# Keys with high and low part in adjacent DRAM rows, and key and query loads that write 128 partitions at once

## The chip, the core and the metric

The kernel runs on one core of a Trainium2 chip. The metric is the device time of one execution in microseconds (us); the time of a kernel is the median of several executions. The engines named below are TensorE (PE in the profile; its weight loads are PEld), VectorE (DVE), ScalarE (ACT), GpSimd (POOL) and SyncE (SP), which issues all DMA transfers of this kernel. Each engine works through its own list of instructions in order.

## The reference

One step of a one-layer encoder over 2048 prompt tokens and 32 sample tokens, with model width 1024. All of it is in float32. What is computed:

```
z = rmsnorm(x) @ w_in                      # columns: q, k, v of group A, then of group B
group A, 4 heads of 2 maps x 64 dims:      # differential attention, 128-dim values
    s = q.k * 64**-0.5 + t5_bias, chunk-causal mask (chunks of 64)
    w = softmax(s[map 1]) - lam * softmax(s[map 2]);   o = w @ v
group B, 8 heads of 64 dims:               # band attention: own chunk and the 8 before it
    s = q.k * 64**-0.5 + clipped relative bias;        o = softmax(s) @ v
h = x + concat(rmsnorm_per_head(oA) * 0.8, rmsnorm(oB)) @ w_out
h = h + square(relu(rmsnorm(h) @ w_up)) @ w_down
h = h + sigmoid(h @ w_ple_gate) * (p @ w_ple_proj)
y = rmsnorm(h)
```

The sample tokens attend to a cache of 128 keys and values beside their own. Keys and values of both groups are outputs too.

## The kernel before, in words

**Precision.** TensorE multiplies in a float32 format (`float32r`) that keeps fewer bits than float32. Each operand is therefore split in a high part and a low part (`split`, L191 to L202): ScalarE copies the value to the high part, and GpSimd or VectorE subtracts to get the low part. A projection multiplies three times (`mm3`, L235 to L241): high by high, high by low, low by high.

**Attention scores use the split differently.** A key has 64 features, and TensorE contracts over 128 partitions. So one key tile holds the high parts of 64 features in partitions 0 to 63 and the low parts in partitions 64 to 127 (`ka` for group A, `kbt` for group B). The query tile `q` holds the same 64 feature rows twice, once in each half of the partitions, and has the query's high part and its low part side by side in its columns. Two matmuls, one with the high and one with the low columns of the query, then give the score with all four products (L669 for group A, L856 for group B).

**Where keys and queries lie.** The projections (`proj`) write them to DRAM scratch: keys to `kS`, laid out as [head, high or low, 128 feature rows, token], queries to `qS`, as [head, map, 64 feature rows, block of 256 tokens, high or low, token]. `caches` adds the cached keys. Attention loads them back:

- `attn_a` (group A, four heads, called for groups `js` of query blocks) loads per head the keys as tiles of up to 1024 tokens, each by one DMA for the high half and one for the low half, and per query block `q` by two DMAs, one for each half of the partitions (`load_q`).
- `attn_b` (group B, eight heads per group of query blocks) loads per head the keys `kbt` by two DMAs and the queries of two blocks by two DMAs, beside the biases `bb` and the values `vbt`.

Each of these loads writes 64 partitions.

**Order of the work.** The program is written in stages: norm and projections of group A for the first half of the tokens; half of differential attention (`JA0`); projections of group B, with half of band attention (`JB`) within; the rest of the projections and of band attention; the other half of differential attention (`JA1`); output projection (`outproj`, matmuls `ops`), MLP (`ups`, `dps`), gate (`gps`) and final norm, block by block of 512 tokens. A scheduler then orders the instructions of each engine by its own model of their times, with the order of the program as priority: where attention has to wait for VectorE or ScalarE, matmuls of later stages (projections, output projection, MLP) stand in between. The change touches what the scheduler sees of the loads, and so the lists of all engines.

**Around 780 to 975 us** band attention of the last blocks and the output projection of the first 512 tokens run side by side. `outproj` makes 8 output tiles; for each it loads a weight tile (`wr`, split by ScalarE into `wh` and by GpSimd into `wl`), loads the residual (`hd`, from `x_t`), lets TensorE do 24 matmuls into `ops`, lets VectorE add them to `hd` (L992), and stores `hd` to `hS`. `oload` brings in attention's result (`oraw`, from `oT`) for the next block and splits it into `oact` or `ou`.

Of the kernel before, what the change touches and what calls it, by code (L numbers as in the profile page):

```python
# [13 lines left out]
F32 = mybir.dt.float32  # L14
# [6 lines left out]
P = 128  # L21
D = 1024
SP = 2048
SS = 32
T = SP + SS
PAST = 128
KC = SP + PAST + SS
# [130 lines left out]
class Kern:  # L158
# [208 lines left out]
    def scratch(self):  # L367
        self.xT = self.a["x_t"]
        self.pT = self.a["p_t"]
        self.qS = self.dram([8, 2, 64, 9, 2, 256], F32, "qS")  # L370
        self.kS = self.dram([8, 2, P, KC], F32, "kS")
        self.vS = [self.dram([KC, D], F32, "vSa"), self.dram([KC, D], F32, "vSb")]
        self.oT = self.dram([P, 8, T], F32, "oT")
        self.hS = self.dram([P, 8, T], F32, "hS")
        self.rS = self.dram([P, T], F32, "rS")
        self.rB = self.dram([P, T], F32, "rB")
# [112 lines left out]
    def proj(self, half, grp, acts, sg, mm, vs=range(2), gs=range(4)):  # L489
# [8 lines left out]
        for g in gs:  # L498
            gi = 4 * grp + g
            for kind in range(2):  # L500
                wh, wl = self.wunit(a["w_qk"][8 * grp + 4 * kind + g], [8, P])
                for b in half:
# [37 lines left out]
                    for i, t in enumerate((hi, lo)):  # L540
                        for c0, kc, n in self.ktok(b):
                            self.dma(self.kS[gi, i, :, kc : kc + n], t[:, c0 : c0 + n])
                    if grp == 0 or b == 3:
# [6 lines left out]
    def caches(self, sg, tp):  # L550
        nc, a = self.nc, self.a
        for grp in range(2):
# [9 lines left out]
            for i, t in enumerate((hi, lo)):  # L562
                self.dma(
                    self.kS[4 * grp : 4 * grp + 4, i, :, SP : SP + PAST].rearrange("g p c -> p g c"),
                    t.rearrange("p (g c) -> p g c", c=P),
                )
            for c in range(2):
                raw = sg.tile([P, 256], F32, tag="vraw", bufs=2, name="cvr")
                self.dma(raw, cv[:, 256 * c : 256 * c + 256])
                hl = sg.tile([P, nh // 2, 2, dv], F32R, tag="vhl", bufs=2, name="cvhl")  # L570
# [7 lines left out]
    def load_q(self, q, gi, ms, j, n=1):  # L578
        for d in range(2):
            dst = q[64 * d : 64 * d + 64]  # L580
            if j is None:
                for i, m in enumerate(ms):
                    self.dma(dst[:, i, :, :SS], self.qS[gi, m, :, 8, :, :SS])
            elif len(ms) == 2:
                self.dma(
                    dst.rearrange("r m l c -> r m (l c)"), self.qS[gi, :, :, j].rearrange("m r l c -> r m (l c)")
                )
            else:
                self.dma(
                    dst.rearrange("r k l c -> r (k l c)"),  # L590
                    self.qS[gi, ms[0], :, j : j + n].rearrange("r k l c -> r (k l c)"),
                )

    def attn_a(self, js, pool, ps_s, ps_t, ps_o):
        nc = self.nc
        last = 8 in js
        nk = SP if last else 256 * (js[-1] + 1)
        late = []
        for g in range(4):
            q = self.queries(g, js[0], pool)  # L600
            kts = [self.kpool.tile([P, 2, 1024], F32R, tag="ka", bufs=2, name="ka") for _ in range(0, nk, 1024)]
            if last:
                ks = pool.tile([P, 2, PAST + SS], F32R, tag="ks", bufs=1, name="ks")
            for hl in range(2):
                src = self.kS[g, hl].rearrange("(m r) c -> r m c", m=2)
                for i, kt in enumerate(kts):
                    c0, n = 1024 * i, min(1024, nk - 1024 * i)
                    self.dma(kt[64 * hl : 64 * hl + 64, :, :n], src[:, :, c0 : c0 + n])
                if last:
                    self.dma(ks[64 * hl : 64 * hl + 64], src[:, :, SP:KC])  # L610
            ba = self.bias_a(self.qpool, g)
            for j in js:
                self.attn_a_pair(g, j if j < 8 else None, kts if j < 8 else [ks], ba, pool, ps_s, ps_t, ps_o, late, q)
                q = None
# [152 lines left out]
    def attn_b(self, js, pool, ps_s, ps_t, ps_o):  # L767
# [12 lines left out]
        for h in range(8):  # L780
            gi, m = 4 + h // 2, h % 2
            bb = self.bias_b(pool, h)
            kt = pool.tile([P, KBW], F32R, tag="kb", bufs=2, name="kbt")
            for hl in range(2):
                self.dma(kt[64 * hl : 64 * hl + 64, : ke - kb], self.kS[gi, hl, 64 * m : 64 * m + 64, kb:ke])
            q = pool.tile([P, 2, 2, 256], F32R, tag="q", bufs=2, name="q")
# [962 lines left out]
```

## Time and profile before

| What | Value |
|---|---|
| Time, median of 3 executions | 3005.77 us (3004.67 to 3011.53) |
| The profiled execution's own time | 3002.77 us |
| Its span, first to last instruction | 3001.0 us |
| TensorE busy | 2903.3 us, 97% |
| VectorE, ScalarE, GpSimd busy | 60%, 58%, 63% |
| Mean granted TensorE clock | 0.993 |
| Bytes moved by DMA | 528.45 MB, mean 176 GB/s |

The profile is of one execution. Its timeline gives for each instruction the start, the duration, the engine, the line, what it writes and reads (`out<-in`), and in brackets how long the engine stood idle ahead of it and what ended that. Its list of waits sums these by pair: who waited for whom, us in total, how often, the longest. A row by stretch gives busy time and count of instructions of PE, PEld, DVE, ACT and POOL, then the granted clock (1.00 is full), the busy share of the core's 16 DMA engines, and GB/s. SPq is SyncE issuing a DMA; the row's duration is the issue, not the transfer. The list of DMA issues gives the count, the size of one, and the median us from issue to landing.

### The profile page before, as it was taken

The numbers are of one execution on the slowest core, as the hardware profiler recorded it, in microseconds if no ns is written. First come the engines' busy times: TensorE is split into PE (matmuls) and PEld (weight loads), VectorE is DVE, ScalarE is ACT, GpSimd is POOL, SyncE is SP. The second block draws the span as 40 slices with busy tenths as digits, with TensorE's granted clock in tenths as the row PEclk, the third lists the DMA queues.
The fourth block names the chain that finished last, engine by engine and source line by source line (L and its number), as shares of the span: only waits on it lengthen the run. The fifth ranks groups of instructions, "written<-read, shape, count | busy, mean of one in ns | idle before, by whom it ended". The sixth has DMA issues, their size and how long they took to land. (4 is left out here: it accounts for less than half of the span.)

```text
span 3001.0 us, 49834 instructions
## 1 busy us (share of the span) xinstructions
PE 2903.3 (97%) x17217; PEld 2567.9 (86%) x17217; DVE 1798.7 (60%) x4147; ACT 1743.6 (58%) x3226; POOL 1877.2 (63%) x2509
## 2 busy tenths in 40 slices
PE   8999999999989999999999999999899999999997
PEld 5888889899877888888888888779788988999997
DVE  5266664676565554667566566445666774677664
ACT  4366555777666665655665655454655555555455
POOL 2578675223465444666655655777687788787774
PEclk9999999999999999999999999999999999999999
DMA  8988777987877453655644543447433456323331
GB/s 284 315 247 246 236 232 210 273 231 225 255 241 219 137 153 108 187 151 170 206 140 127 150 148 106 164 136 230 158 99 134 129 168 244 122 85 121 102 102 52
DMA packets 295204, 528.45 MB, mean 176 GB/s; under 512 B 36316, under 2 KB 159232, under 8 KB 294952
## 3 DMA queue, kind: packets, MB, share of 16 engines
q1 hardware_dynamic: 294952, 525.27, 56.3%
q8 instruction: 136, 2.23, 0.3%
q14 instruction: 116, 0.95, 0.1%
HBM read 424.66 MB, written 104.45 MB: 176 GB/s over the span
## 5 line engine op out<-in xcount | busy, mean ns | idle before, releaser
L191 POOL TENSOR_TENSOR wl<-wr,wh 128x256 fp32r<-128x256 f32 x632 | 472.8, 781 | 278.5 <-ACT wh L196 241.2
L196 ACT ACTIVATE piece<-wr 128x512 fp32r<-128x512 f32 x406 | 247.2, 625 | 268.9 <-PE ups L240 123.3
L191 POOL TENSOR_TENSOR piece<-wr,piece 128x256 fp32r<-128x256 f32 x404 | 340.2, 870 | 91.2 <-ACT piece L196 82.5
L196 ACT ACTIVATE wh<-wr 128x1024 fp32r<-128x1024 f32 x228 | 240.3, 1056 | 198.1 <-PE ups L240 43.0
L181 POOL TENSOR_TENSOR wl<-wr,wh 128x256 fp32r<-128x256 f32 x280 | 216.0, 804 | 202.8 <-ACT wh L196 202.7
L241 PE MATMUL dps<-uh,piece 128*128 128x272 f32 (+1 forms) x768 | 245.6, 323 | 3.6 <-POOL piece L181 3.5
L239 PE MATMUL dps<-uh,piece 128*128 128x272 f32 (+1 forms) x768 | 244.3, 322 | 4.2 <-ACT piece L196 2.6
L241 PE MATMUL ups<-cs,piece 128*128 128x256 f32 (+1 forms) x864 | 246.8, 286 | 0.0
L240 PE MATMUL ups<-cs,piece 128*128 128x256 f32 (+1 forms) x864 | 246.2, 285 | 0.0
L240 PE MATMUL dps<-ul,piece 128*128 128x272 f32 (+1 forms) x768 | 246.0, 322 | 0.0
L239 PE MATMUL ups<-cs,piece 128*128 128x256 f32 (+1 forms) x864 | 246.0, 285 | 0.0
L181 POOL TENSOR_TENSOR piece<-wr,piece 128x256 fp32r<-128x256 f32 x280 | 229.9, 854 | 12.9 <-ACT piece L196 11.7
L239 PE MATMUL qps<-aH,wh 128*128 128x512 f32 (+1 forms) x640 | 225.6, 352 | 3.3 <-DVE kr L526 1.8
L240 PE MATMUL qps<-aL,wh 128*128 128x512 f32 (+1 forms) x640 | 225.5, 352 | 0.0
L241 PE MATMUL qps<-aH,wl 128*128 128x512 f32 (+1 forms) x640 | 225.3, 352 | 0.0
L684 ACT ACTIVATE e<-e,nm 128x128 f32<-128x128 f32 (+16 forms) x136 | 157.1, 1155 | 113.2 <-DVE nm L682 113.0
L1181 DVE TENSOR_TENSOR h<-h,dps 128x512 f32<-128x512 f32 x256 | 172.9, 681 | 68.4 <-PE dps L241 67.3
L239 PE MATMUL dps<-uh,wh 128*128 128x512 f32 x512 | 204.5, 400 | 5.2 <-DVE h L1181 4.6
L239 PE MATMUL ups<-cH,wh 128*128 128x512 f32 x512 | 201.9, 395 | 0.0
L241 PE MATMUL ups<-cH,wl 128*128 128x512 f32 x512 | 201.6, 394 | 0.0
L240 PE MATMUL ups<-cL,wh 128*128 128x512 f32 x512 | 201.6, 394 | 0.0
L241 PE MATMUL dps<-uh,wl 128*128 128x512 f32 x512 | 200.8, 392 | 0.0
(313 smaller groups left out, 9075.4 us busy)
## 6 DMA issues: line engine op xcount, KB each, us to landing
wr<-w_up SPq DMA_DIRECT2D x128, 512.0 KB, 3.5
wr<-w_down SPq DMA_DIRECT2D x128, 512.0 KB, 3.7
v<-vSa SPq DMA_DIRECT2D x64, 512.0 KB, 4.6
q<-qS SPq DMA_DIRECT2D x128, 256.0 KB, 5.4
wr<-w_qk SPq DMA_DIRECT2D x50, 512.0 KB, 4.9
ka<-kS SPq DMA_DIRECT2D x32, 512.0 KB, 7.4
wr<-w_out SPq DMA_DIRECT2D x32, 512.0 KB, 4.3
wr<-w_ple_gate SPq DMA_DIRECT2D x32, 512.0 KB, 3.9
```

The lines of the kernel that those rows point to most:

```text
L181: nc.gpsimd.tensor_tensor(out[:, sl], a[:, sl], b[:, sl], op=op)
L191: nc.gpsimd.tensor_tensor(out[:, sl], a[:, sl], b[:, sl], op=op)
L196: nc.scalar.activation(hi, raw, AF.Copy)
L239: nc.tensor.matmul(ps, lh, rh, start=start and i == 0, stop=False)
L240: nc.tensor.matmul(ps, lh, rl, start=False, stop=False)
L241: nc.tensor.matmul(ps, ll, rh, start=False, stop=stop and i == n - 1)
L684: nc.scalar.activation(row, row, AF.Exp, bias=nmx, accum_out=z[:nr, m : m + 1])
L1181: nc.vector.tensor_tensor(hv, hv, ps, op=ALU.add)
```

## The change

Keys lie in `kS` as [head, 128 feature rows, high or low, token]: the high and the low part of a feature stand in adjacent rows. The stores change their row address alone. A key tile is loaded by one DMA whose source rows run through feature and part together, so partition 2r holds the high part of feature r and partition 2r + 1 its low part. The query tile must match: feature row r goes to partitions 2r and 2r + 1, by one DMA that names each source row twice (`twice`). For group A a query load is one DMA for each of the two maps, where it was one for each half of the partitions; for group B one DMA where there were two. Tiles, matmuls and all other arithmetic stay.

```diff
-        self.kS = self.dram([8, 2, P, KC], F32, "kS")
+        self.kS = self.dram([8, P, 2, KC], F32, "kS")
...
-                            self.dma(self.kS[gi, i, :, kc : kc + n], t[:, c0 : c0 + n])
+                            self.dma(self.kS[gi, :, i, kc : kc + n], t[:, c0 : c0 + n])
...
     def load_q(self, q, gi, ms, j, n=1):
-        for d in range(2):
-            dst = q[64 * d : 64 * d + 64]
+        def twice(dst, src):
+            self.dma(dst, src.unsqueeze(1).broadcast_to((64, 2, src.shape[1])))
+
+        for i, m in enumerate(ms):
             if j is None:
-                for i, m in enumerate(ms):
-                    self.dma(dst[:, i, :, :SS], self.qS[gi, m, :, 8, :, :SS])
+                for x in range(2):
+                    twice(q[:, i, x, :SS], self.qS[gi, m, :, 8, x, :SS])
             elif len(ms) == 2:
-                self.dma(
-                    dst.rearrange("r m l c -> r m (l c)"), self.qS[gi, :, :, j].rearrange("m r l c -> r m (l c)")
-                )
+                twice(q[:, i].rearrange("p l c -> p (l c)"), self.qS[gi, m, :, j].rearrange("r l c -> r (l c)"))
             else:
-                self.dma(
-                    dst.rearrange("r k l c -> r (k l c)"),
-                    self.qS[gi, ms[0], :, j : j + n].rearrange("r k l c -> r (k l c)"),
+                twice(
+                    q.rearrange("p k l c -> p (k l c)"),
+                    self.qS[gi, m, :, j : j + n].rearrange("r k l c -> r (k l c)"),
                 )
...
-            for hl in range(2):
-                src = self.kS[g, hl].rearrange("(m r) c -> r m c", m=2)
-                for i, kt in enumerate(kts):
-                    c0, n = 1024 * i, min(1024, nk - 1024 * i)
-                    self.dma(kt[64 * hl : 64 * hl + 64, :, :n], src[:, :, c0 : c0 + n])
-                if last:
-                    self.dma(ks[64 * hl : 64 * hl + 64], src[:, :, SP:KC])
+            src = self.kS[g].rearrange("(m r) x c -> (r x) m c", m=2)
+            for i, kt in enumerate(kts):
+                c0, n = 1024 * i, min(1024, nk - 1024 * i)
+                self.dma(kt[:, :, :n], src[:, :, c0 : c0 + n])
+            if last:
+                self.dma(ks, src[:, :, SP:KC])
...
-            for hl in range(2):
-                self.dma(kt[64 * hl : 64 * hl + 64, : ke - kb], self.kS[gi, hl, 64 * m : 64 * m + 64, kb:ke])
+            self.dma(kt[:, : ke - kb], self.kS[gi, 64 * m : 64 * m + 64, :, kb:ke].rearrange("r x c -> (r x) c"))
```

The number of DMA instructions falls from 1509 to 1417; the counts of all other engines' instructions stay. The scheduler puts them in another order: about a quarter of TensorE's matmuls stand some places earlier or later, nearly all between the end of the first half of differential attention and the first third of the second half. From the middle of that half on, TensorE's list is the same but for one place. Two places show it. A row is line, operation, `out<-in`, and the shape of what is written; x2 means twice in a row.

SyncE's list, behind the load of `oraws` (attention's result for the second block), ahead of the residual loads `hd` of the first output tiles. Before:

```order
L172 DMA kbt<-kS 64x1024 x2
L172 DMA q<-qS 64x1024 x2
L172 DMA q<-qS 64x2x512 x2
L172 DMA bb<-dbb 128x640
L172 DMA ka<-kS 64x2x1024
L172 DMA ka<-kS 64x2x512
L172 DMA ka<-kS 64x2x1024
L172 DMA ka<-kS 64x2x512
L172 DMA ba<-dba 128x256
L172 DMA q<-qS 64x2x512
L172 DMA vbt<-vSb 128x8x128
L172 DMA q<-qS 64x2x512
```

Two stores of `hd`, the next load of `hd` and a load of `wr` follow. After:

```order
L172 DMA q<-qS 128x1x512 x2
L172 DMA ka<-kS 128x2x1024
L172 DMA ka<-kS 128x2x512
L172 DMA ba<-dba 128x256
L172 DMA q<-qS 128x1x512 x2
L172 DMA kbt<-kS 128x1024
L172 DMA q<-qS 128x1x1024
L172 DMA bb<-dbb 128x640
L172 DMA hS<-hd 128x512 x2
L172 DMA hd<-x_t 128x512
L172 DMA wr<-w_out 128x1024 x2
L172 DMA vbt<-vSb 128x8x128
```

The loads of group A went ahead of those of the band head, each pair of loads became one, and the values `vbt` moved behind the residual and the weights.

TensorE's list at the end of one output tile of `ops` and the start of the next one, which is the first `ops` row to need a new `wh`. Before:

```order
L240 MATMUL ops<-oact,wh 128x512
L241 MATMUL ops<-oact,wl 128x512
L856 MATMUL sb<-kbt,q 128x320 x4
L914 MATMUL ob<-pb,vbt 128x512 x4
L914 MATMUL ob<-pb,vbt 128x2x128 x2
L884 MATMUL tpb<-ident,eb 128x128 x5
L239 MATMUL ops<-oact,wh 128x512
L240 MATMUL ops<-oact,wh 128x512
L241 MATMUL ops<-oact,wl 128x512
```

Here `sb` are scores, `ob` the product with the values, `tpb` transposed weights of the band attention, all of one step; the new output tile starts behind it. After (lines are two lower):

```order
L241 MATMUL ops<-oact,wl 128x512
L239 MATMUL ops<-oact,wh 128x512
L240 MATMUL ops<-oact,wh 128x512
L854 MATMUL sb<-kbt,q 128x320 x2
L241 MATMUL ops<-oact,wl 128x512
L239 MATMUL ops<-oact,wh 128x512
L240 MATMUL ops<-oact,wh 128x512
L241 MATMUL ops<-oact,wl 128x512
L239 MATMUL ops<-oact,wh 128x512
L240 MATMUL ops<-oact,wh 128x512
L854 MATMUL sb<-kbt,q 128x320 x2
```

The new tile starts in the second row, directly behind the old one's last, and the attention step's matmuls stand in pairs behind its start.

More of the change, by code (lines that the diff above doesn't have):

```diff
@@ L563, in caches @@
                 self.dma(
-                    self.kS[4 * grp : 4 * grp + 4, i, :, SP : SP + PAST].rearrange("g p c -> p g c"),
+                    self.kS[4 * grp : 4 * grp + 4, :, i, SP : SP + PAST].rearrange("g p c -> p g c"),
                     t.rearrange("p (g c) -> p g c", c=P),
```

## The prediction

> **What bounds the kernel now.** I read the page's shares first, then the stages of the span, then who makes TensorE wait in each, and last the DMA queue where those waits are.
>
> ```profile
> PE 2903.3 (97%) x17217; PEld 2567.9 (86%) x17217; DVE 1798.7 (60%) x4147; ACT 1743.6 (58%) x3226; POOL 1877.2 (63%) x2509
> ```
>
> TensorE is busy for 2903.3 of 3001.0 us. The change leaves every matmul as it is (same count, same shapes), so what it can move is the 97.7 us in which TensorE is idle, and the clock. By stage (columns: the stretch and its length, then busy us and count of each engine, granted clock, DMA share, GB/s):
>
> ```profile
> 0.00:450.00 450.00, 426.27 (x2388) 365.27 (x2389) 253.96 (x634) 244.12 (x489) 285.91 (x395) 1.00 0.82 260
> 450.00:780.00 330.00, 319.92 (x2297) 300.66 (x2295) 192.16 (x692) 224.54 (x488) 126.00 (x205) 1.00 0.81 234
> 780.00:975.00 195.00, 176.52 (x852) 145.13 (x851) 113.09 (x319) 128.14 (x243) 110.36 (x155) 0.97 0.81 241
> 975.00:1875.00 900.00, 896.92 (x4654) 759.76 (x4652) 547.84 (x1391) 550.92 (x909) 507.06 (x716) 1.00 0.50 149
> ```
>
> Band attention runs in the second and third stretch, half of the differential attention in the fourth. There TensorE is idle for 3.1 us in 900: it always has MLP matmuls to fill with, so loads that land sooner buy nothing in it. After 1875 us nothing of keys or queries is loaded. The idle time that this change can reach is the 10.1 us of the second stretch and the 18.5 us of the third, both with DMA engines 81% busy. TensorE's waits in the third, by who ended them (us in total, times, longest):
>
> ```profile
> PE ops L239 <- ACT wh L196: 4.9, 2, 4.6
> PE sb L856 <- DVE stb L859: 4.4, 3, 1.8
> PE ops L239 <- DMA oraw<-oT: 3.3, 1, 3.3
> PE ops L240 <- DVE oact L202: 1.9, 1, 1.9
> PE ops L239 <- ACT oact L196: 1.8, 1, 1.8
> ```
>
> And from 496 to 620 us, the first heads of band attention:
>
> ```profile
> PE sb L856 <- issue: 1.5, 1, 1.5
> ...
> PE sb L856 <- DMA qS<-ql: 1.0, 1, 1.0
> PE sb L856 <- DMA q<-qS: 1.0, 2, 0.7
> ```
>
> TensorE hardly waits for a key or query load itself. The 4.6 us wait looks like ScalarE's, but the timeline shows what stood behind it. The DMA queue (start, us, what it issues):
>
> ```profile
> 799.79 1.09 SPq L172 DMA_DIRECT2D kbt<-kS  x2
> 800.93 2.53 SPq L172 DMA_DIRECT2D q<-qS  x4
> 804.05 0.33 SPq L172 DMA_DIRECT2D bb<-dbb  x1
> 804.48 2.55 SPq L172 DMA_DIRECT2D ka<-kS  x4
> ...
> 816.32 0.33 SPq L172 DMA_DIRECT2D hd<-x_t  x1
> ```
>
> VectorE, ScalarE and TensorE behind it, with the idle time ahead of each and what ended it in brackets:
>
> ```profile
> 824.24 0.69 DVE L992 TENSOR_TENSOR hd<-hd,ops 128x512 f32<-128x512 f32 x1 [6.80 <-DMA hd<-x_t]
> 825.02 0.63 ACT L997 ACTIVATE tmp<-hd 128x512 f32<-128x512 f32 x1 [6.62 <-DVE stb L865]
> 826.28 1.99 ACT L196 ACTIVATE wh<-wr 128x1024 fp32r<-128x1024 f32 x2
> 827.37 0.79 PE L239 MATMUL ops<-oact,wh 128*128 128x512 f32 x1 [4.64 <-ACT wh L196]
> ...
> 856.81 0.50 PE L239 MATMUL ops<-oact,wh 128*128 128x512 f32 x1 [3.33 <-DMA oraw<-oT]
> ```
>
> A burst of key and query loads is issued from 799.8 us. The residual tile hd, issued behind it at 816.3, is still missing when VectorE needs it; VectorE stands for 6.8 us, ScalarE behind it for 6.6, and so the weights' high part wh, which only had to be copied, comes 4.64 us late. Two stretches of that burst show why it is slow:
>
> ```profile
> 800.00:816.00 16.00, 16.00 (x82) 13.29 (x82) 8.54 (x26) 12.16 (x24) 12.29 (x19) 1.00 0.95 220
> 821.00:826.50 5.50, 1.73 (x12) 1.32 (x10) 0.76 (x2) 1.48 (x3) 0.77 (x2) 1.00 0.98 382
> 826.83:830.24 3.41, 2.87 (x7) 2.17 (x8) 1.98 (x7) 3.10 (x6) 3.16 (x6) 0.50 0.32 117
> 857.55:860.96 3.41, 3.41 (x13) 2.93 (x13) 2.94 (x8) 2.53 (x6) 0.00 (x0) 0.50 0.76 276
> ```
>
> With the DMA engines equally busy, the 64-partition loads move 220 GB/s and the 128-partition transfers behind them (hd, wr, vbt, hS) 382. The last two rows are the half clock that follows the waits that end at 827.4 and 856.8.
>
> **The change, part by part.**
>
> Stores of keys: the same instructions, with twice the row pitch in DRAM; runs stay 512 elements long. I cost this at nothing, covered by the other rows of the queue; a price of its own is not shown, and its bounds are ±0.5 us, the size of one issue.
>
> Fewer issues. Key loads fall from two per tile to one, band query loads likewise (the differential ones stay two): 24 + 32 + 4 + 32 = 92 issues go.
>
> ```profile
> L172 SPq DMA_DIRECT2D q<-qS x128: 444/594/2967, 97.5 to 1751.4; - x128
> L172 SPq DMA_DIRECT2D kbt<-kS x64: 444/472/1297, 496.6 to 1104.7; - x64
> ```
>
> At 0.47 to 0.59 us that is 43 to 54 us of the DMA queue. The queue is not on TensorE's path except where it runs without a pause, in the first heads of band attention, where TensorE's "issue", qS and q waits above make 3.5 us. I take half, **-1.7**; ends 0 and -3.5.
>
> The burst at 800 us. It holds these, per the list of DMA issues of 798 to 830 us:
>
> ```profile
> q<-qS SPq DMA_DIRECT2D x6, 256.0 KB, 5.8
> ka<-kS SPq DMA_DIRECT2D x2, 512.0 KB, 10.5
> kbt<-kS SPq DMA_DIRECT2D x2, 256.0 KB, 3.8
> ka<-kS SPq DMA_DIRECT2D x2, 256.0 KB, 9.8
> vbt<-vSb SPq DMA_DIRECT2D x1, 512.0 KB, 12.4
> ```
>
> 6 x 256 + 2 x 512 + 4 x 256 = 3584 KB, 3.67 MB: 16.7 us at 220 GB/s, 9.6 at 382, so 7.1 us sooner. In the new order the 512 KB of vbt stand behind hd and wr, another 1.4 us at 382. Against it: TensorE's own order puts the start of the next output tile ahead of an attention step that it used to follow, and that step covered
>
> ```profile
> 820.27 0.75 PE L856 MATMUL sb<-kbt,q 128*128 128x320 f32 x4
> 820.86 1.33 PE L914 MATMUL ob<-pb,vbt 128*128 128x512 f32 x6
> 822.03 0.71 PE L884 MATMUL tpb<-ident,eb 128*128 128x128 f32 x5
> ```
>
> 2.8 us. Net 7.1 + 1.4 - 2.8 = 5.7, over the 4.64: the wait goes, **-4.6**. Ends: all of it, or, if the loads are no faster, +2.8. No row prices a 128-partition load whose source names each query row twice; its ends are the two rates above, and I take 382, because that stretch is nearest in what the change makes of these loads, a write to all 128 partitions. With the wait goes the half clock from 826.8 to 830.2: 3.41 us at half speed is 1.7 us of matmul time, **-1.7** (ends 0 and -1.7). The Trainium skill, "TensorE: Matmul & The Clock Gate", Part 1, says that the clock falls to half after an idle window of about 3.4 us. By that rule the 3.3 us wait before 856.8 would cost no clock; the trace has half clock right after it, so the row decides, and the sum by the page alone would be 0.9 us smaller.
>
> The waits for oraw and oact (3.3, 1.9, 1.8). Each stands behind the next head's two kbt and two q loads, 1024 KB: 4.8 us at 220, 2.7 at 382, 2.0 sooner. I take **-2.0** of the 3.3, with half of its clock window **-0.9**, and half of each of the others, **-1.8** together. Ends: 0, and all, -8.7.
>
> VectorE's part in the waits of sb (4.4). In the third stretch VectorE stands for the residual tile and TensorE for VectorE:
>
> ```profile
> DVE hd L992 <- DMA hd<-x_t: 19.3, 6, 6.8
> ```
>
> If a third of those 4.4 us goes with it, **-1.5**; ends 0 and -4.4.
>
> New waits. The orders of TensorE, VectorE and ScalarE shift by some tens of places between 175 and 1335 us, and in one place near 2000. A step that now stands ahead of its data costs about what the sb waits cost, 4.4 / 3 = 1.5 us; I allow a bit over one such wait, **+2.0**, ends 0 and +20.
>
> Sum: -1.7 - 4.6 - 1.7 - 2.0 - 0.9 - 1.8 - 1.5 + 2.0 = -12.2 us. Everything before 975 us passes to the end undiminished, since the fill work of the fourth stretch is the same. The profiled execution took 3002.77 us, 3.0 less than the median of the runs shown, 3005.77; the forecast for a median is 3005.77 - 12.2 = 2993.6, say 2994. What is next late is the residual load behind its own store, and VectorE in the band steps.
>
> **The rivals.**
>
> Hidden anyway. For: in the whole trace TensorE waited 2.5 us for q and never for a key tile, and when one wait in a list-ordered queue closes the next one takes over (VectorE's 4.4 us are attention's own chain). Against: the 6.8 us that VectorE stands for a residual load are DMA time and nothing else. It gives the issue term, -1.7, and about as much of new waits: 3004 to 3006. The same time comes out if the change does not do what it says, because the engines and not the destination set the pace. The Trainium skill, "DMA: Bandwidth & Descriptors", section "Rules for kernel authors", says that a load issued early and waited for late overlaps with compute; by that rule alone the change would give this rival's 3004 to 3006. The trace agrees for the key and query loads themselves (2.5 us), and not for what queues behind them (6.8 us). The waits for q:
>
> ```profile
>   PE sb L856: 2.5, 3
> ```
>
> Slower: the order. The place is 780 to 850 us, where the start of an output tile now stands ahead of the attention step. If hd and wr come less than 2.8 us sooner, TensorE meets every such seam with less cover: the eight output tiles of this block times 2.8 less what they gain. It decides from a gain per load of about 1 us (1.8 x 8 = 14): 3006 + 14 - 2, some 3018. For: list order is rigid, one late load holds all behind it. Against: 7.1 us of relief at the worst place.
>
> Large gain. All of the idle time of the third stretch that the rows above name (16.3), both clock windows (3.4) and the 3.5 of the second go: -23, 2983. For: all of it stands in stretches with DMA at 81%. Against: the waits for stb are short and many.
>
> **How the numbers follow.** 0.3% of 3005.77 is 9.0 us, about what a measurement of this kernel can tell from no change; faster means below 2996.7, slower above 3014.8. Forecast, 52%: -5 to -17 us, two thirds of it beyond 9. Large gain, 15%. Hidden, 21%. Slower, 12%. Faster: 0.35 + 0.15 = 0.50. Same: 0.17 + 0.21 = 0.38. Slower 0.12. The range takes the large gain's middle at one end (2981) and reaches past the hidden case at the other (3010); it leaves out most of the slower case and a bit of the large gain, 0.15 in all.
>
> **What would show it.** Right: the burst at 800 us moves 350 GB/s or more, VectorE's wait for hd falls from 19.3 to under 10, the clock column of the third stretch rises to 0.99, its TensorE idle time falls from 18.5 to about 9; the fourth stretch stays at 3 us. Wrong: the burst stays near 220 GB/s; or it is fast and the idle time of the third stretch stands at other lines; or idle time appears after 975 us, where I count none.

## The result, and the profile after

| | Before | After |
|---|---|---|
| Median beside each other | 3006.15 us (3004.67 to 3011.53) | 2976.26 us (2970.37 to 2979.25) |
| Ratio, 95% interval | | 0.9887 (0.9866 to 0.9907) |
| Profiled execution, its span | 3002.77, 3001.0 us | 2970.37, 2968.6 us |

The changed kernel is 1.1% faster, some 30 us at the medians. Measured twice more beside the kernel before it gave 0.9916 (0.9901 to 0.9931) and 0.9888 (0.9868 to 0.9908); the mean of the three, 0.9897, is used below. The forecast was 2994, 12 us faster, with 2981 as the lower end of the range. The direction came as forecast; the gain is two and a half times as large, and the time lies outside the range.

The shares of the engines in the changed kernel's page:

```profile
PE 2901.2 (98%) x17217; PEld 2567.8 (86%) x17217; DVE 1801.7 (61%) x4147; ACT 1745.1 (59%) x3226; POOL 1878.8 (63%) x2509
```

TensorE does the same work in the same busy time (2903.3 before), so the 32.4 us by which the span is shorter are idle time: 97.7 us before, 2968.6 - 2901.2 = 67.4 after. The same stretches as before, columns as there:

```profile
0.00:450.00 450.00, 431.78 (x2418) 370.45 (x2419) 255.90 (x642) 247.28 (x493) 285.12 (x395) 1.00 0.79 261
450.00:780.00 330.00, 325.95 (x2319) 304.92 (x2317) 201.16 (x703) 230.24 (x501) 130.46 (x212) 1.00 0.76 245
780.00:975.00 195.00, 190.01 (x934) 156.91 (x934) 117.29 (x345) 136.35 (x259) 116.79 (x170) 0.99 0.73 240
975.00:1875.00 900.00, 898.84 (x4657) 761.91 (x4656) 540.61 (x1360) 546.31 (x901) 514.88 (x728) 1.00 0.45 147
```

Idle time of TensorE falls from 23.7 to 18.2 us, from 10.1 to 4.1, from 18.5 to 5.0 and from 3.1 to 1.2. The DMA engines carry about as many GB/s as before and are busy for less of the time doing so: 0.76 and 0.73 of it in the second and third stretch, where it was 0.81. Over the whole span the row of SyncE's queue (packets, MB, and the time of the packets as a share of 16 engines' span) says the same. First the kernel before:

```profile
q1 hardware_dynamic: 294952, 525.27, 56.3%
```

And the changed kernel:

```profile
q1 hardware_dynamic: 293480, 525.27, 53.3%
```

56.3% of 3001.0 is 1690 us, 53.3% of 2968.6 is 1582: the same bytes in 108 us less of all 16 engines. That is one execution of each. A kernel with the new layout and the old loads (below) has 1652, and two more executions of the changed kernel have 1554 and 1560, so the size of the saving is uncertain; that there is one is not.

The burst at 800 us is now issued like this (start, us, what):

```profile
784.08 5.69 SPq L172 DMA_DIRECT2D ka<-kS  x2
...
793.25 0.34 SPq L172 DMA_DIRECT2D kbt<-kS  x1
793.63 0.51 SPq L172 DMA_DIRECT2D q<-qS  x1
...
796.41 0.48 SPq L172 DMA_DIRECT2D hd<-x_t  x1
797.00 2.87 SPq L172 DMA_DIRECT2D wr<-w_out  x2
```

The rates of two stretches of it, same columns as the stretches above:

```profile
783.00:799.00 16.00, 15.82 (x78) 12.99 (x77) 10.28 (x33) 13.65 (x26) 10.34 (x15) 1.00 0.88 282
799.00:803.00 4.00, 4.00 (x22) 3.43 (x22) 1.28 (x6) 1.18 (x4) 2.28 (x6) 1.00 1.01 391
```

The residual tile hd is issued 20 us sooner than before (796.4 for 816.3), behind loads that move 282 GB/s with the engines 88% busy, where it was 220 at 95%. Most of the 20 us is that the whole burst begins 17 us sooner: its first load is issued at 782.8, where it was 799.8, and TensorE is 11 us further on by then. From the burst's first load to hd it is 13.6 us, where it was 16.5. TensorE's waits in the changed kernel, 780 to 975 us (who ended them; us in total, times, longest):

```profile
PE sb L854 <- DVE stb L857: 1.4, 3, 1.0
PE ops L240 <- DVE oact L202: 1.1, 1, 1.1
PE ops L239 <- ACT oact L196: 1.1, 3, 0.6
...
PE ops L239 <- ACT wh L196: 0.2, 1, 0.2
```

The wait of 4.6 us for wh and the one of 3.3 us for oraw are gone, and none of that size took their place. VectorE's wait for the residual tile in the same stretch:

```profile
DVE hd L990 <- DMA hd<-x_t: 10.8, 6, 2.9
```

It was 19.3, the longest 6.8; in the two further executions of the changed kernel it is 11.5. What the prediction didn't look at is the second stretch from VectorE's side. In the kernel before, from 450 to 780 us, VectorE stood for these transfers:

```profile
DVE vhl L198 <- DMA vSa<-vhl: 5.6, 3, 2.8
DVE ql L521 <- DMA qS<-ql: 5.5, 2, 3.1
```

In the changed kernel:

```profile
DVE t L916 <- DMA qS<-qh: 2.4, 1, 2.4
DVE ql L521 <- DMA qS<-ql: 1.7, 2, 1.4
DVE ql L521 <- DMA kS<-ql: 0.9, 1, 0.9
```

Stores of the projections' values (`vhl`) and queries (`ql`) wait in the same queue behind the key and query loads. VectorE waits until they have landed before it writes the next tiles, and attention's steps on VectorE stand behind that in its list. 11.1 us of such waits became 5.0. TensorE's own waits name little of this (1.0 us for a store of `ql`, shown in the prediction). From 490 to 620 us in the kernel before, 3.5 us were for the queue or a transfer, which the prediction shows, and these were for VectorE's and ScalarE's steps:

```profile
PE tpb L884 <- DVE pb L893: 2.3, 4, 0.6
PE qps L239 <- DVE ql L521: 1.5, 1, 1.5
...
PE sb L856 <- DVE stb L859: 1.3, 2, 0.8
PE ob L914 <- ACT eb L864: 1.2, 1, 1.2
```

In the changed kernel this is left, 2.4 us in all:

```profile
PE qps L239 <- DVE ql L521: 1.4, 1, 1.4
PE tpb L882 <- DVE pb L891: 0.7, 2, 0.5
PE sb L854 <- DVE stb L857: 0.3, 1, 0.3
```

So all of the 3.5 us went, and 3.9 of the 6.3. That VectorE's waits for the stores are how the transfers reach those steps is argued and not shown: from 488 to 614 us the kernels that gain nothing have 8.3 to 10.5 us of these waits and most that gain have 0.9 to 5.8, but one that gains 4.8 us there still has 8.0 (Wide, half the columns).

**Where the time went, stretch by stretch.** For each kernel the start of TensorE's n-th matmul was read from the trace and the same number's start in the kernel before subtracted. The bounds are the n-th matmul's time in the kernel before. The table gives what each stretch gains (-) or loses (+), in us. It is one execution against one, and the first row of the experiments (Layout only), with the same lists of instructions as the kernel before, shows how far chance alone goes: up to 4 us in a stretch.

| Kernel | 0 to 301 | to 403 | to 488 | to 614 | to 784 | to 1008 | to 1483 | to the end | Sum |
|---|---|---|---|---|---|---|---|---|---|
| Forecast | 0 | 0 | 0 | -1.7 | 0 | -12.5 | 0 | +2.0 | -12.2 |
| Changed, first | -0.7 | -2.9 | +0.4 | -8.7 | +0.5 | -15.7 | -3.5 | -1.8 | -32.4 |
| Changed, second | +0.6 | -2.5 | +0.6 | -8.7 | +0.6 | -12.7 | -2.5 | 0.0 | -24.6 |
| Changed, third | -0.5 | -3.0 | +0.6 | -8.0 | +0.3 | -14.3 | -3.3 | -1.9 | -30.1 |
| Layout only | +3.8 | -0.9 | 0.0 | +0.9 | -0.2 | +3.6 | -1.3 | +1.8 | +7.7 |
| Band loads wide | +2.2 | -1.7 | 0.0 | -8.2 | +0.6 | -14.4 | +0.7 | +3.7 | -17.1 |
| Group A loads wide | +0.7 | -2.9 | +0.2 | 0.0 | -0.2 | -3.7 | -2.6 | -3.3 | -11.8 |
| Wide, half the columns | -0.1 | -2.4 | 0.0 | -4.8 | -1.5 | -12.6 | -1.3 | +3.4 | -19.3 |
| Wide, with a sliver | +0.6 | +4.0 | -0.1 | -6.3 | -1.5 | -6.6 | -4.8 | +6.6 | -8.1 |
| Two halves of 64 | +7.1 | +1.7 | -1.7 | +4.6 | 0.0 | +0.9 | -2.4 | +7.8 | +18.0 |

(The +2.0 of the forecast, for new waits, had no place of its own.)

### The profile page after: what moved, and what is told of

The parts are those of the page before. It is cut to its first block, busy times and chain, and to the rows that moved or that the text cites. A ratio compares the mean times of both kernels' runs of the same rounds, so it can differ in the third digit from the quotient of the medians.

```text
span 2968.6 us, 49743 instructions
## 1 busy us (share of the span) xinstructions
PE 2901.2 (98%) x17217; PEld 2567.8 (86%) x17217; DVE 1801.7 (61%) x4147; ACT 1745.1 (59%) x3226; POOL 1878.8 (63%) x2509
## 3 DMA queue, kind: packets, MB, share of 16 engines
q1 hardware_dynamic: 293480, 525.27, 53.3%
## 4 chain that ended last, share of the span: by engine, by line
PE 83%; DMA 5%; DVE 4%; POOL 3%; ACT 2%; issue 2%; SPq 0%; DVEq 0%; POOLq 0%; ACTq 0%
PE dps L241 8%; PE dps L239 8%; PE dps L240 8%; PE ups L239 7%; PE ups L240 7%; PE ups L241 7%; PE s L668 4%; PE qps L239 3%; PE qps L241 3%; PE qps L240 3%; PE ob L912 2%; PE tpp L733 2%; PE tpb L882 2%; PE gps L241 2%; PE sb L854 2%
## 5 line engine op out<-in xcount | busy, mean ns | idle before, releaser
L181 POOL TENSOR_TENSOR piece<-wr,piece 128x256 fp32r<-128x256 f32 x280 | 232.2, 861 | 13.2 <-ACT piece L196 11.8
L240 PE MATMUL dps<-ul,wh 128*128 128x512 f32 x512 | 201.3, 393 | 0.0
```

The costliest lines, as they stand in the source:

```text
L181: nc.gpsimd.tensor_tensor(out[:, sl], a[:, sl], b[:, sl], op=op)
L240: nc.tensor.matmul(ps, lh, rl, start=False, stop=False)
```

## The experiments

Three theories stood against each other. Width: one transfer that writes 128 partitions occupies the DMA engines for less time than two that write 64 each, and what queues behind it lands sooner. Issues: 92 fewer DMA instructions relieve SyncE. Order: the scheduler's new lists are better by themselves. Nearly every kernel here gets lists of its own from the scheduler, so Order is set aside only where the lists are equal for a stretch; what is said below of lists is the order of the instructions in the traces.

**Layout only.** The new order of rows in DRAM, with loads of 64 partitions as before; the lists are those of the kernel before.

```diff
-                src = self.kS[g, hl].rearrange("(m r) c -> r m c", m=2)
+                src = self.kS[g, :, hl].rearrange("(m r) c -> r m c", m=2)
...
-                self.dma(kt[64 * hl : 64 * hl + 64, : ke - kb], self.kS[gi, hl, 64 * m : 64 * m + 64, kb:ke])
+                self.dma(kt[64 * hl : 64 * hl + 64, : ke - kb], self.kS[gi, 64 * m : 64 * m + 64, hl, kb:ke])
```

> Keys in DRAM as in the change, but tiles and loads as before: 64 partitions each, 1509 DMAs, and every engine's list in the order of before. Three theories of the 30 us. Width: a load that writes 128 partitions takes about half the DMA engines' time, and all that queues behind it lands sooner. Issues: 92 fewer DMA instructions free SyncE's list. Order: the scheduler's new lists are better by themselves. All three expect no change here, 3000 to 3012; a gain of 5 us or more would put part of it on the layout in DRAM.

Measured: 3005.54 us, ratio 0.999 (0.9979 to 1.0002). The stretches that matter are as before:

```profile
450.00:780.00 330.00, 320.10 (x2295) 301.71 (x2294) 192.59 (x693) 222.71 (x485) 127.19 (x208) 0.99 0.79 233
780.00:975.00 195.00, 174.07 (x839) 142.64 (x838) 110.16 (x309) 127.28 (x241) 105.06 (x146) 0.96 0.81 243
```

Where the rows lie in DRAM is worth nothing that this run can tell from zero, which is what the prediction had for the stores. TensorE's wait for wh in the third stretch is there as before, in a second execution with the old lists and loads:

```profile
PE ops L239 <- ACT wh L196: 4.9, 2, 4.6
```

**Band loads wide.** Only `kbt` and the band queries are loaded as in the changed kernel; group A's loads write 64 partitions.

```diff
     def load_q(self, q, gi, ms, j, n=1):
+        if len(ms) == 2:
+            for d in range(2):
+                dst = q[64 * d : 64 * d + 64]
...
-            src = self.kS[g].rearrange("(m r) x c -> (r x) m c", m=2)
...
+            for hl in range(2):
+                src = self.kS[g, :, hl].rearrange("(m r) c -> r m c", m=2)
```

> Only band attention (kbt and its q) loads 128 partitions at once, differential attention loads as before; 1445 DMAs; the lists are nearly those of the changed kernel (542 of 17212 matmuls stand elsewhere). Width: the waits of 490 to 620 us go (8 us) and most of those of 780 to 975, but the key burst of group A near 790 us stays slow and keeps a wait of 2 to 5 us: 2980 to 2990. Order: as the changed kernel, 2973 to 2981. Issues: two thirds of the gain, 2984 to 2988.

Measured: 2986.67 us, ratio 0.9925 (0.9906 to 0.9944), about 23 us faster.

```profile
450.00:780.00 330.00, 326.54 (x2333) 305.82 (x2333) 200.17 (x702) 230.21 (x499) 130.73 (x213) 1.00 0.74 243
780.00:975.00 195.00, 188.11 (x927) 155.57 (x926) 119.56 (x342) 135.98 (x257) 113.42 (x164) 0.99 0.73 240
```

Idle time of 3.5 and 6.9 us and a DMA share of 0.74 and 0.73: the band's loads, with the lists that come with them, make the gain of both stretches. The total fits Width (2980 to 2990) and Issues (2984 to 2988) alike, and is beyond Order (2973 to 2981). VectorE's waits for stores in the second stretch are those of the changed kernel:

```profile
DVE t L934 <- DMA qS<-qh: 2.4, 1, 2.4
DVE ql L521 <- DMA qS<-ql: 2.1, 2, 1.5
```

From 488 us on TensorE, VectorE and ScalarE have the changed kernel's lists here. By the table it gains nothing from 1008 to 1483 us (+0.7), where the changed kernel gains about 3: the lists are equal, so that difference speaks for group A's loads, though a stretch can differ by as much by chance.

**Group A loads wide.** The other half alone: `ka`, `ks` and group A's queries as in the changed kernel, `kbt` and the band queries with 64 partitions. From 470 to 1480 us the lists of TensorE, VectorE, ScalarE and GpSimd are those of the kernel before (the expectation below has TensorE's equal from 420 us; they are not before 470).

```diff
     def load_q(self, q, gi, ms, j, n=1):
+        if len(ms) == 1:
+            for d in range(2):
+                dst = q[64 * d : 64 * d + 64]
...
-            self.dma(kt[:, : ke - kb], self.kS[gi, 64 * m : 64 * m + 64, :, kb:ke].rearrange("r x c -> (r x) c"))
+            for hl in range(2):
+                self.dma(kt[64 * hl : 64 * hl + 64, : ke - kb], self.kS[gi, 64 * m : 64 * m + 64, hl, kb:ke])
```

> Only differential attention (ka, ks and its q) loads 128 partitions at once, band attention loads as before; 1481 DMAs; the lists are nearly those of before (544 of 17212 matmuls stand elsewhere, none of them between 420 and 975 us). Width: of the 3.67 MB of the burst at 800 us 2.6 MB load at the high rate, 5 us sooner, so the 4.6 us wait at 822 us and its half clock go, and the 3 us between 370 and 403: 2993 to 2999. Order: in that stretch nothing changes, the wait stays, 3001 to 3006. Issues: a third of the gain or less, and none at 822 us: 2997 to 3004.

Measured: 2991.09 us, ratio 0.9955 (0.9939 to 0.9971), about 13 us faster, and 2 us below what Width expected. The second stretch and the third, then TensorE's waits in the third:

```profile
450.00:780.00 330.00, 319.02 (x2285) 299.63 (x2282) 191.97 (x690) 225.99 (x491) 127.33 (x207) 1.00 0.80 234
780.00:975.00 195.00, 180.18 (x873) 147.00 (x872) 115.25 (x324) 129.11 (x245) 109.81 (x158) 0.98 0.77 241
```

```profile
PE sb L872 <- DVE stb L875: 7.1, 4, 5.6
...
PE ops L239 <- ACT wh L196: 0.2, 1, 0.2
```

With the same lists as before, the wait of 4.6 us for wh is gone. Four loads of `ka` ahead of hd and wr had become two that write 128 partitions; hd is issued at 811.1 us instead of 816.3, and VectorE's longest wait for it is 4.4 us, where it was 6.8. So on this wait the loads act without Order. The stretch as a whole gains 3.7 us (784 to 1008), no more than chance makes. The long wait for VectorE, 5.6 us, is no effect of the loads: the layout-only kernel, with the same lists, has one of 5.3 there, and stands 7.3 us behind this one in the stretch. The second stretch, whose loads are the band's, stays as before (idle 11.0 us, DMA share 0.80), and VectorE's waits there are the same as before:

```profile
DVE vhl L198 <- DMA vSa<-vhl: 5.6, 3, 2.8
DVE ql L521 <- DMA qS<-ql: 5.5, 2, 3.0
```

The gain to 403 us and from 1008 to 1483 us, -2.9 and -2.6, is there, as in the changed kernel; the latter is not there with the band's loads alone. Of the former, kernels with the old loads and lists there show -0.9 (Layout only) and -1.7 (Band loads wide) too.

**Wide, half the columns.** All loads write 128 partitions, each cut in two DMAs of half the columns (the two maps for `ka`, the two query blocks for `q`, tokens for `kbt`): 1509 DMAs, the number before.

```diff
-                self.dma(kt[:, :, :n], src[:, :, c0 : c0 + n])
+                    self.dma(kt[:, m, :n], src[:, m, c0 : c0 + n])
```

> All loads write 128 partitions, but each in two DMAs of half the columns, so that the number of DMAs is that of before, 1509; the lists differ from both kernels (2991 matmuls from before, 4045 from the changed one). Width: 2973 to 2984. Issues: no gain, 3000 to 3010. Order: anything, as these lists are a third kind.

Measured: 2983.08 us, ratio 0.9917 (0.9901 to 0.9934). With as many DMAs as the layout-only kernel, 1509, it is 0.9990 - 0.9917 = 0.0073 faster, 22 us, so a smaller number of issues is not what makes the gain. Width expected 2973 to 2984, Issues 3000 to 3010. Its lists are those of the kernel before up to 488 us and a third kind behind that, so Order isn't excluded by this run alone. It stands 0.0020 behind the changed kernel, 6 us, less than the intervals can tell.

**The changed kernel again**, for the spread of its own result.

> The changed kernel once more, on the chip and beside the runs of before that the next three share. All theories: 2968 to 2982.

Measured: 2978.62 us (2978.18 to 2979.37), ratio 0.9916 (0.9901 to 0.9931).

**Small DMAs added.** The changed kernel with a DMA of 16 elements, from DRAM to DRAM, behind each merged load, to take the 92 issues saved back.

```diff
+    def extra(self, elems):
+        self.nd += 1
+        i = self.nd % 64
+        self.dma(self.xD[self.nd, i : i + 1, :16], self.zD[0, i : i + 1, 0, :16])
```

> The changed kernel with 92 tiny DMAs added (64 bytes, DRAM to DRAM, one beside each load that was merged), so that SyncE issues 1509 DMAs again; the lists are those of the changed kernel but for 10 matmuls. Nothing of the result is changed. Width: no more than 3 us over the changed kernel, 2973 to 2980. Issues: a third or more of the 30 us comes back, 2986 to 3006. Order: no change.

Measured: 3008.63 us, ratio 1.0006 (0.9994 to 1.0018). It did not test what it meant to. No tile holds these copies where the loads are, so the scheduler put all of them at the start. The first row is the copies' issues, the other two are waits of TensorE from 0 to 170 us, which the kernel before does not have:

```profile
L172 SPq DMA_DIRECT2D xD<-w_up x92: 488/580/1941, 18.1 to 169.0; - x92
...
PE pa L321 <- DMA ta<-t_table: 8.1, 1, 8.1
PE qps L239 <- DVE ql L524: 7.0, 2, 5.4
```

At TensorE's 600th matmul (156 us in the kernel before) it is 29.9 us late; from there to 1422 us it gains 30.3 and draws level, as the changed kernel does. So the gain of the change does not hang on the number of issues elsewhere; but 92 issues of 0.58 us, 53 us of SyncE, cost 30 us in the first 170 us.

**Large DMAs added.** The same with copies of 160 to 512 KB, 45 MB in all.

```diff
+        x = self.zD[u].rearrange("p k c -> p (k c)")
+        self.dma(self.xD[self.nd, :, :elems], x[:, :elems])
```

> The changed kernel with the same 92 DMAs grown to copies of 160 to 512 KB in DRAM, some 45 MB in all, which at 382 GB/s is 117 us of the DMA engines, about what the wide loads saved; the lists are those of the changed kernel but for 542 matmuls. Nothing of the result is changed. Width (the freed DMA time is the cause): most of the gain is lost, 2992 to 3010. Issues: as the tiny DMAs. Order: the gain stays, 2973 to 2982.

Measured: 3099.9 us, ratio 1.0319 (1.0304 to 1.0334), with the copies at the start again. It says only that 45 MB there cost some 120 us; for the change nothing follows. Width had expected 2992 to 3010.

**Stores merged.** The changed layout makes the high and the low part of a key tile one block, so one DMA can store both (1377 DMAs).

```diff
-                    for i, t in enumerate((hi, lo)):
-                        for c0, kc, n in self.ktok(b):
-                            self.dma(self.kS[gi, :, i, kc : kc + n], t[:, c0 : c0 + n])
+                    for c0, kc, n in self.ktok(b):
+                        self.dma(self.kS[gi, :, :, kc : kc + n], hl[:, :, c0 : c0 + n])
```

> The changed kernel with the high and low part of a key in one tile and stored by one DMA where there were two, 40 DMAs fewer; 3601 matmuls stand elsewhere. Width: the bytes and the rate stay, -2 to +3 us against the changed kernel. Issues: 40 of 92 of what the change itself gave, 5 us or more faster, below 2972. Order: anything within 10 us.

Measured: 2974.14 us, ratio 0.9903 (0.9886 to 0.992), where the changed kernel beside it had 0.9916. Issues had expected less than 2972. The intervals overlap, so both were run again, below.

**Wide, with a sliver.** To add issues that the tiles do hold in place: each load of 128 partitions is cut in all but its last 16 columns and the last 16.

```diff
-                self.dma(kt[:, :, :n], src[:, :, c0 : c0 + n])
+                self.dma(kt[:, :, : n - 16], src[:, :, c0 : c0 + n - 16])
+                self.dma(kt[:, :, n - 16 : n], src[:, :, c0 + n - 16 : c0 + n])
```

> The changed kernel with each key and query load cut in two unequal pieces, both over all 128 partitions: all but the last 16 columns, and the last 16. 1601 DMA issues instead of 1417, 92 more than the kernel before has; the bytes are the same, and the tiles' waits hold each piece where its load was. Width: full-width writes are kept, so most of the gain stays; the extra issues cost at most a few us, at the heads of band attention (487 to 615 us), where the halved-columns variant lost 4 us: 2979 to 2988. Issues: if fewer issues made the gain, 184 more lose all of it and more: 3006 or above.

Measured: 2991.2 us, ratio 0.9957 (0.9942 to 0.9972). The kernel keeps 13 us of the gain and loses 0.0060, 18 us, against the changed kernel. That is more than Width allowed (2988) and far less than Issues needed (3006). Put down to the 184 issues more, it would be about 0.1 us each; that is an estimate, since its lists differ from the changed kernel's too (about a quarter of TensorE's matmuls).

```profile
450.00:780.00 330.00, 325.89 (x2351) 307.03 (x2349) 197.16 (x707) 231.22 (x501) 126.55 (x210) 1.00 0.76 243
780.00:975.00 195.00, 184.16 (x883) 151.80 (x883) 113.47 (x315) 129.81 (x242) 112.09 (x161) 0.97 0.72 241
```

The DMA share is the changed kernel's (0.76, 0.72), so the slivers don't load the engines; the idle time of the third stretch is 10.8 us. One part of this run sets Order aside: from 519 to 600 us of the kernel before, the lists of TensorE, VectorE, ScalarE and GpSimd are those of the kernel before, and 4.5 of the 6.3 us that it gains from 488 to 614 are gained there. Two kernels with the same lists and narrow loads of the band gain 0.3 (Layout only) and 0.6 (Group A loads wide) there.

**Two halves of 64.** About the same number of DMAs, 1605, but each load cut by partitions, 0 to 63 and 64 to 127, with the layouts and the doubled rows of the changed kernel kept.

```diff
-                self.dma(kt[:, :, :n], src[:, :, c0 : c0 + n])
+            for d in (slice(0, 64), slice(64, P)):
...
+                    self.dma(kt[d, :, :n], src[d, :, c0 : c0 + n])
```

> The changed kernel with its layouts in DRAM and in the tiles kept (rows of high and low part interleaved, each query row named twice in the source), but each load cut in two DMAs of 64 partitions, as before: 1605 issues. Width: the loads are slow again, so the gain is gone: 3000 to 3015, with VectorE's waits for the residual tile hd back near 19 us in 780 to 975 us (10.8 in the changed kernel), and its waits for stores of vhl back at 3 us or more in 487 to 620 (none in the changed kernel). Layout: if interleaving or the doubled source rows make the loads fast, it stays within 10 us of the changed kernel: 2979 to 2989. Order: its lists differ from both kernels' by some 9000 matmuls' places, so the time would lie outside both, by an amount that the lists set.

Measured: 3020.96 us, ratio 1.0049 (1.0032 to 1.0065): 30 us slower than the sliver kernel beside it, with the same rows, bytes and, but for four, issues, and 6 us slower than Width expected. It is the nearest that the runs come to Width alone, but the lists differ. The stretches, then VectorE's waits for hd and for the stores of vhl, 450 to 975 us:

```profile
450.00:780.00 330.00, 319.42 (x2274) 299.70 (x2274) 190.94 (x685) 221.94 (x483) 123.08 (x205) 0.99 0.77 229
780.00:975.00 195.00, 176.33 (x866) 145.62 (x865) 112.16 (x324) 129.13 (x246) 99.40 (x144) 0.96 0.81 250
```

```profile
DVE hd L995 <- DMA hd<-x_t: 14.0, 8, 5.3
...
DVE vhl L198 <- DMA vSa<-vhl: 8.4, 3, 3.5
```

Idle time is back at 10.6 and 18.7 us, the waits for vhl at 8.4; those for hd at 14.0, not 19. Its lists differ from those of all the others (about half of TensorE's matmuls stand elsewhere than in the kernel before), and 7 of its 18 us are lost before 301 us, where 56 of its 312 loads of this kind are issued; that part may be Order. Against the sliver kernel, 18.4 of the 26.1 us between the two executions lie from 488 to 614 and from 784 to 1008 us, where the band's loads are. The time that the queue's packets took (its share times the span) follows the width in all kernels, whatever their lists: 1690 and 1652 us (the kernel before, Layout only) and 1633 (this one) with all loads narrow, 1605 and 1596 with half of them wide, 1550 to 1582 with all of them wide (half the columns, sliver, the changed kernel three times, merged stores twice). The Trainium skill, "SBUF — State Buffer", section "Can I just issue two DMAs to hit both halves?", says no: two transfers on partitions 0 and 64 queue on the same engines, and only one transfer over all 128 partitions reaches all ports. The trace agrees on the rate, with 220 GB/s for the pairs (engines 95% busy) and 282 for what replaced them (88%); no run here shows the ports.

**Merged stores and the changed kernel once more**, beside each other.

> The changed kernel with the high and the low part of a block's keys held in one tile and stored by one DMA instead of two (40 issues fewer, 1377), once more and beside the changed kernel, in more rounds. By the cost per issue that the 184 added ones showed (12.6 us, 0.07 us each), 40 fewer are worth 3 us: 2974 to 2977 where the changed kernel takes 2978, a ratio to the kernel before that is 0.001 lower. If issues of stores cost nothing, the two are equal.

> The changed kernel itself, as the other side of this comparison: 2975 to 2980, ratio 0.989 to 0.992.

Measured: merged stores 2978.05 us, 0.9893 (0.9875 to 0.9911); the changed kernel 2975.07 us, 0.9888 (0.9868 to 0.9908). Merging the stores gives no gain that could be shown; 3 us were expected if each issue costs 0.07 us.

## Why the prediction was right and where it was wrong

**Right: the mechanism of the third stretch, and in part by luck its sum.** The burst was slow with loads of 64 partitions, the residual tile stood behind it, and wide loads take the wait for wh away, with the old lists too. The terms of that stretch (-4.6, -1.7, -2.0, -0.9, -1.8, -1.5) sum to -12.5; the three executions gave -12.7 to -15.7. Its idle time was to fall to about 9 us and fell to 5.0, 8.5 and 7.6; the clock was to rise to 0.99 and did. The terms that were taken as halves or a third, those for oraw, oact and sb, were nearly wholes: of 16.3 us named, 3.8 are left. The size of the first term has a wrong working: at the measured 282 GB/s the burst is only 3.7 us shorter, and 3.7 + 1.4 - 2.8 = 2.3 us would not have covered the 4.64. The wait went all the same; the burst's earlier start, which the prediction did not have, may be why. No run has the new lists with narrow loads, so how the stretch's 14 us divide between Width and Order stays open; with other lists and wide loads it gains 12.6 (half the columns) and 6.6 (sliver).

**Wrong: the term "Fewer issues", as the only one of the second stretch.** The prediction counted 10.1 us of idle time there as within reach, and then priced 3.5 of them, those that TensorE waited for by the name of the queue or of a load; it took half, -1.7. Measured: -8.0 to -8.7 from 488 to 614 us. All of the 3.5 went, and with it 3.9 of the 6.3 us that stood at VectorE's and ScalarE's steps of attention; the prediction took such waits for attention's own chain (it says so of VectorE's 4.4 us, in the rival "Hidden anyway"). Nor was it the number of issues: the sliver kernel, with 92 more of them than the kernel before, gains 6.3 there, 4.5 of it with equal lists. It is the width of the band's loads: with them narrow the stretch gains nothing, with them wide 4.8 to 8.7. A row that hints at the way, VectorE standing for stores of vhl and ql, was in the profile of before: 11.1 us with the band's loads narrow (Group A loads wide), 4.5 with them wide (Band loads wide). Whether those waits are the way stays open, since the changed kernel's executions have 5.0, 3.3 and 8.4 us of them at nearly the same gain. This step is 7 of the 17 us missing.

**Wrong: "loads that land sooner buy nothing" in the fourth stretch, and no term for the differential attention of the first.** They gave -2.5 to -3.5 and -2.5 to -3.0. Group A's loads alone gave -2.6 and -2.9 there, which is at the edge of what single executions can tell. For the fourth stretch the band-wide kernel, with the changed kernel's lists and no gain, speaks for the loads, and TensorE's idle time fell from 3.1 us to 1.2, 2.0 and 1.3. For the first, kernels with the old loads and lists show -0.9 and -1.7, so only 1 to 2 us of it can be put down to the change.

**Wrong: the allowance of +2.0 for new waits.** None of size came; the seams of the eight output tiles, the rival "Slower", have 0.2 us of waits for wh (1.0 and 0.8 in the two further executions).

Taken as means of the three executions, the second stretch makes -6.8 more than forecast, the first -2.8, the fourth -3.1, the allowance -2.0 and the third stretch -1.7, together -16.4. With the forecast's -12.2 that is -28.6, where the mean of the three spans is 29.0 shorter.

**Perhaps too small: an issue's price.** Taken at nothing wherever the queue pauses, it came to at most about 0.1 us each in the sliver kernel, if all of that kernel's loss is put down to issues. By that estimate the 92 issues saved would be 9 us, by the half-columns kernel 6; the width, with the lists that came with it, 22 to 30. The parts need not add up, and the intervals, of some 5 us each, don't allow a finer split. **Open** stays what four of the kernels with more DMAs than the changed one lose after 1483 us (+3.4 to +7.8), where little of this is loaded.

**What was to show it.** "The burst moves 350 GB/s or more" failed as put: it is spread out now, 282 GB/s over 16 us; 391 stands only in the 4 us behind, when the stores of hd and the loads of hd and wr move. "The wait for hd under 10" was missed closely, 10.8. "Idle time appears after 975 us" did not happen. "Large gain", -23, was the rival nearest to what came, and too small for the same reason: it summed what was named in two stretches, 3.5 us of the second, and left two out.

## What to carry to other kernels

Two loads that write 64 partitions each are not one load that writes 128. Here, where DMA was busy for four fifths of a stretch, merging them won back much of the idle time that stood there, under whatever name (10.1 us to 4.1, 18.5 to 5.0). To price a faster transfer, list what every engine waits for from the same queue, stores that free tiles included, and follow each to TensorE; its own waits name the last engine in the chain only. An issue may not be free where the queue is dense: 92 of them at the start cost 30 us, though in place 184 cost 18 at most. And before a gain is put down to a change, compare the lists: a scheduler that reorders is a second change.

## What was not expected of the hardware

**A source that names each row twice shows no penalty.** The medians from issue to landing, changed kernel:

```profile
q<-qS SPq DMA_DIRECT2D x64, 256.0 KB, 4.3
ka<-kS SPq DMA_DIRECT2D x16, 1024.0 KB, 6.9
```

A query load of 256 KB took 5.4 us before with plain rows and 64 partitions. Key loads of twice the size land sooner than the halves did (512 KB, 7.4 us before). These times contain waiting in the queue, so they are no rates.

**The half clock without a long gap.** The changed kernel has one such window left in the third stretch, and the one ahead of it:

```profile
835.59:839.00 3.41, 1.98 (x12) 1.29 (x11) 2.75 (x11) 2.12 (x6) 3.41 (x6) 1.00 0.92 322
839.00:842.41 3.41, 3.13 (x11) 2.46 (x10) 3.06 (x7) 2.59 (x5) 0.71 (x2) 0.50 0.82 232
```

TensorE was busy for 1.98 of 3.41 us, with no idle gap over 0.98, and half clock followed. In the kernel before, a window with less work had full clock behind it:

```profile
939.47:942.88 3.41, 1.64 (x8) 1.02 (x6) 1.59 (x7) 0.81 (x2) 0.32 (x3) 1.00 1.07 369
942.88:946.29 3.41, 2.79 (x16) 2.10 (x15) 3.38 (x8) 2.62 (x5) 1.84 (x2) 1.00 0.32 97
```

That window has an idle gap of 1.77 us. So neither the length of a gap nor the busy time of a window tells it here; what does stays open. The Trainium skill, "TensorE: Matmul & The Clock Gate", Part 1, has the clock fall after an idle window of about 3.4 us; here it fell with no such window, and the rows decide.
